# First stage of a hybrid retention and gMLP kernel: squares of x and context taken in the feature layout, and the first loads in another order

## The chip, the cores and the metric

The kernel runs on one core of a Trainium2 chip. The metric is the device time of one execution in microseconds. A second number, the span, is the time from the first to the last instruction of a profiled execution.

## The reference

The model has two layers over 512 latent tokens x and 256 context tokens ctx, each of 1024 features. Layer 0 mixes tokens by bidirectional retention, layer 1 by a chunked gMLP. The part that matters here is the beginning of layer 0: both streams are normalised over their features, modulated by vectors made from `c` and `c_ctx`, and multiplied with the input weights.

```python
def rmsnorm(x, g):
    xf = x.astype(F32)
    y = xf * lax.rsqrt(jnp.mean(xf * xf, axis=-1, keepdims=True) + NORM_EPS)
    return (y * g.astype(F32)).astype(x.dtype)
...
        shift_x, scale_x, gate_x = jnp.split(silu_c @ ada_w[i] + ada_b[i], 3, axis=-1)
        shift_c, scale_c, gate_c = jnp.split(silu_cc @ ada_w[i] + ada_b[i], 3, axis=-1)
        hx = rmsnorm(x, norm_g[i]) * (1 + scale_x[:, None]) + shift_x[:, None]
        hc = rmsnorm(ctx, norm_g[i]) * (1 + scale_c) + shift_c
...
    q = to_heads(h @ w_in[:, :a], RET_HEADS)
    k = to_heads(h @ w_in[:, a:bq], RET_HEADS) * (RET_QK_DIM ** -0.5)
```

So each token needs the sum of its 1024 squared features, and each feature needs a scale and a shift.

## The kernel before, in words

**Layout.** x and ctx lie with features on the partitions: 1024 features are eight blocks of 128, called kb (0 to 7), and tokens run along the free axis. x stands in four tiles `xq[th, g]` (128 x 4 x 256): th is the half of the tokens, g the half of the feature blocks. ctx stands in two tiles `cq[g]`. Layer 0's modulation weights come in eight pairs `ada_w[kb]`, 1 MB each.

**Precision.** Every float32 operand is cut into a high part (type fp32r, made by ScalarE, `act.copy` or an activation) and a low part (made by VectorE, source minus high part), and `mm3` (line 110) makes a product of three TensorE instructions: low times high, high times low, high times high. So each operand needs one pass of ScalarE and one of VectorE before TensorE can use it. In `features` (line 306) the first of the three needs the low part of the weights and the high part of x, the second needs the low part of x.

**The first stage** (lines 419 to 766) makes k and q of head 0 as a plain product: for each kb and each token half th, 12 TensorE instructions (`plain(kb, th)`, line 664), for the context 6. Around a block stand: `ada0_mm(kb)` (line 535), eight float32 products of the modulation with `ada_w[kb]`, and a copy by ScalarE; `ada0_cols(kb, e)` (line 545), two transposes that turn the result to the partitions, then a reduce and three small instructions on VectorE that leave scale `gs0` and shift `sh0`; `come(...)` (line 639), which scales a block of x or ctx by scale and reciprocal root (VectorE), adds the shift and makes the high part (ScalarE) and the low part (VectorE). The weight pieces of head 0 are items 0 to 3 of the stream `Q` (line 139); `Q.upto(n)` cuts items into high and low parts, 128 x 1024 at a time. Its tiles `hl` have four buffers, so items 4 and 5, the first of the second stage, take buffers that items 0 to 3 leave.

**The sums of squares** (`flips` and `squares`, lines 510 to 519): TensorE transposes 128 x 128 pieces of x into PSUM so that tokens lie on the partitions, and ScalarE squares them with a running sum per partition. `inverse` (line 521) adds the two halves, takes the root and the reciprocal; `spread` (line 526) multiplies a broadcast of the 128 reciprocals with the identity matrix so that they lie along the free axis on every partition, and ScalarE copies the result to `rs[th]`. The two halves of x are treated one after the other (`by_half`), the context's flips stand behind blocks 2 and 3, its spread behind block 4, and its blocks go through `come` and `plain` in the groups of `CTX_COME` and `CTX_PLAIN` (lines 729, 730).

**What sets the order.** In this stage `pe`, `act` and `dve` keep the order of the text (`kept`, lines 419 and 480, until line 766): each instruction of TensorE, ScalarE and VectorE goes behind the one before it in the text. Afterwards only TensorE does, and a scheduler orders the other two. Loads go out on SyncE's queue in the order of the text (`load`, line 128), those of `Q` when a slot is free (`pump`). `fill(n)` (line 464) issues n products of ones that nobody reads. Nearly every instruction is recorded at line 55, the helper that issues it.

The second stage begins with head pair (0, 1) of v, in the trace the first products of the form pst<-hl,oA.

Of the kernel before, what the change touches and what calls it, by code (L numbers as in the profile page):

```python
# [14 lines left out]
P = 128  # L15
D = 1024
# [52 lines left out]
def hybrid_kernel(ctx, tc, xT_d, cT_d, cv_d, sv_d, rows_d, ada0_d, adag_d, w_d, rope_d, dec_d, ws_d, id_d, out_d):  # L69
# [69 lines left out]
    class Stream:  # L139
# [3 lines left out]
        def __init__(self):  # L143
            self.items, self.loads, self.raws, self.left, self.tiles = [], [], {}, {}, {}
            self.free, self.stage, self.done, self.sent, self.at = [], 0, 0, 0, -1
            self.gate = self.limit = self.cap = None

# [10 lines left out]
        def load(self, key, slots, stage, parts):  # L158
            self.loads.append((key, slots, stage, parts))

# [274 lines left out]
    ADA_AT = ("oS1", "oS2", "oS4", "oA22", "oS1", "oS2", "oS4", ("w4", "g1"))  # L435
# [12 lines left out]
    load(xq[0, 0], xT_d[:, 0:4, 0:HS])  # L448
    load(ident, id_d)
    load(xq[0, 1], xT_d[:, 4:8, 0:HS])  # L450
    load(sv, sv_d)
    ada0_load(0)
    Q.stage = 1
    Q.pump_n(1)
    load_x(1)
    Q.pump_n(1)
    for kb in (1, 2, 3):
        ada0_load(kb)
    for g in range(2):
        load(cq[g], cT_d[:, 4 * g:4 * g + 4, :])  # L460
# [49 lines left out]
    def squares(pq, s):  # L510
        act.activation(t2("junk0"), pq, AF.Square, accum_out=s)

    def flips(src, g, i, s):

        pq = pt()
        for k in range(4):
            pe.transpose(pq[:, k * P:k * P + P], src(4 * g + k, i), ident)
        squares(pq, s[:, g, i:i + 1])
        return pq

    def inverse(s):
        dve.tensor_tensor(s[:, 0, :], s[:, 0, :], s[:, 1, :], ALU.add)
        act.activation(s[:, 1, :], s[:, 0, :], AF.Sqrt, bias=eps, scale=1.0 / D)
        dve.reciprocal(s[:, 1, :], s[:, 1, :])

    def spread(s, name):

        pr = pt((P, HS), tag="tm")
        for i in range(2):
            mm(pr[:, i * P:i * P + P], s[:, 1, i:i + 1].to_broadcast([P, P]), ident, start=True, stop=True)  # L530
# [14 lines left out]
    def ada0_cols(kb, e):  # L545
# [6 lines left out]
        dve.tensor_tensor(gs0[:, kb, :], s[:, 0, :], adab0[:, 1, kb, :], ALU.add)  # L552
        dve.tensor_tensor(sh0[:, kb, :], s[:, 1, :], adab0[:, 0, kb, :], ALU.add)
        dve.scalar_tensor_tensor(gs0[:, kb, :], gs0[:, kb, :], 1.0, g0[:, kb, :], ALU.add, ALU.mult)
# [70 lines left out]
    def half_rows(src, g, s):  # L625
        for i in range(2):
            flips(src, g, i, s)

    def by_half(src, name, n=0):
        s = sq[name] = st([P, 2, 2], f"sq{name}", name="sq")  # L630
        for g in range(2):
            half_rows(src, g, s)
            if g == 0:
                fill(n)
# [62 lines left out]
    for low in lows:  # L697
        low()
# [927 lines left out]
```

## Time and profile before

| what | value |
|---|---|
| runs of before, median (lowest to highest) | 875.29 us (875.2 to 875.54) |
| the profiled execution: time | 875.18 us |
| the profiled execution: span | 873.4 us |
| TensorE busy | 862.0 us, 99% of the span |
| VectorE busy | 708.6 us, 81% |
| ScalarE busy | 472.3 us, 54% |
| loads and stores | 153.80 MB, mean 176 GB/s |
| mean granted TensorE clock | 0.999 |

In a row of the timeline stand the start in us, the duration, the engine, the line, the operation, the output and its inputs, the shape and the count, and in brackets how long the engine was idle before and what ended that. PE is TensorE's matrix product, PEld its weight load, DVE is VectorE, ACT ScalarE, SPq SyncE's queue of loads. The trace shows a float32 product as two PE and two PEld records. In a row of stretches stand the stretch, its length, the busy time of PE, PEld, DVE, ACT and POOL with counts, then the granted clock, the share of the DMA engines and GB/s. In a row of groups stand the count, the busy time, the mean duration in ns and the idle time before.

### The profile page before, as it was taken

The page shows a single profiled execution, that of the slowest core. Times are in us where ns is not written, and L with a number is a line of the kernel's source. Part 1 is how long each engine was busy: PE and PEld are TensorE (multiplying, and loading weights), DVE is VectorE, ACT ScalarE, POOL GpSimd, SP SyncE. Part 2 cuts the span into 40 slices and gives each one's busy share as a digit, 9 for nine tenths or more (in the row PEclk, how much of TensorE's full clock was granted, in tenths as well). Part 3 has the DMA queues.
Part 4 walks back from the last instruction along what each step waited for, and adds up shares of the span by engine and source line. Part 5 has one row for each costly group of instructions (what it writes and reads, how often), then busy time and mean ns, then how long its engine had stood idle before and what let it go on. Part 6 is the DMA issues. An engine that isn't in the chain of part 4 may idle for free.

```text
span 873.4 us, 14635 instructions
## 1 busy us (share of the span) xinstructions
PE 862.0 (99%) x5670; PEld 777.3 (89%) x5670; DVE 708.6 (81%) x998; ACT 472.3 (54%) x763; POOL 62.6 (7%) x100
## 2 busy tenths in 40 slices
PE   8999999999999999999999999999999999999996
PEld 6898899898889888999989898888999899899895
DVE  2689979988696987878688869978898578779976
ACT  5466444553524576536362559785865455255345
POOL 0000210110121020000000010102000000000200
PEclk9999999999999999999999999999999999999999
DMA  9941761972695596758175722446435045045602
GB/s 332 393 136 62 241 219 59 301 253 97 213 370 145 192 314 220 258 167 303 42 254 188 232 85 77 146 167 217 146 122 176 17 146 191 7 142 194 94 28 97
DMA packets 77094, 153.80 MB, mean 176 GB/s; under 512 B 8032, under 2 KB 35040, under 8 KB 77024
## 3 DMA queue, kind: packets, MB, share of 16 engines
q1 hardware_dynamic: 68736, 128.53, 44.6%
q0 software_dynamic: 8000, 24.13, 8.4%
q8 instruction: 44, 0.72, 0.3%
q14 instruction: 26, 0.21, 0.1%
q10 hardware_dynamic: 288, 0.20, 0.1%
HBM read 128.71 MB, written 24.12 MB: 175 GB/s over the span
## 4 chain that ended last, share of the span: by engine, by line
PE 93%; ACT 2%; DVE 2%; DMA 2%; issue 0%; SPq 0%; ACTq 0%
PE pst L55 93%; DMA xq<-in_xT_dram 2%; DVE hl L55 1%; ACT hl L55 1%; ACT f L55 1%; ACT oA L55 0%; ACT junk L55 0%; DVE o L55 0%; DVE xq L55 0%; ACT o L55 0%; DVE cq L55 0%; DVE raw L55 0%; ACT oS L55 0%; DVE gs L55 0%; ACT fss L55 0%
## 5 line engine op out<-in xcount | busy, mean ns | idle before, releaser
L55 DVE TENSOR_TENSOR hl<-raw,hl 128x1024 fp32r<-128x1024 f32 x195 | 237.3, 1223 | 71.8 <-ACT hl L55 71.1
L55 ACT CAST hl<-raw 128x1024 fp32r<-128x1024 f32 x195 | 203.6, 1049 | 156.9 <-DVE raw L55 63.1
L55 PE MATMUL pst<-oS,hl 128*128 128x256 f32 x1104 | 134.1, 280 | 0.5 <-ACT oS L55 0.4
L55 PE MATMUL pst<-hl,oS 128*128 128x512 f32 x576 | 134.2, 390 | 0.1
L55 PEld LDWEIGHTS pst<-oS,hl 128*128 128x128 f32 x1104 | 130.9, 188 | 1.3 <-ACT oS L55 0.9
L55 PEld LDWEIGHTS pst<-hl,oS 128*128 128x128 f32 x576 | 107.9, 188 | 23.2 <-DVE oS L55 0.5
L55 PE MATMUL pst<-oA,hl 128*128 128x256 f32 x936 | 117.8, 281 | 0.2
L55 PEld LDWEIGHTS pst<-oA,hl 128*128 128x128 f32 x936 | 112.7, 188 | 2.4 <-issue 0.4
L55 DVE TENSOR_TENSOR raw<-raw 128x1024 f32<-128x1024 f32 x92 | 111.5, 1222 | 0.9
L55 PE MATMUL pst<-hl,oA 128*128 128x512 f32 x408 | 95.8, 390 | 0.0
L55 PE MATMUL pst<-og,hl 128*128 128x256 f32 x768 | 92.8, 280 | 0.0
L55 PEld LDWEIGHTS pst<-og,hl 128*128 128x128 f32 x768 | 90.9, 188 | 0.8 <-issue 0.4
L55 PEld LDWEIGHTS pst<-hl,oA 128*128 128x128 f32 x408 | 76.2, 188 | 15.5
L55 ACT COPY snap<-pst 128x512 f32<-128x512 f32 x84 | 49.1, 585 | 43.0 <-PE pst L55 41.9
L55 PE MATMUL pst<-hl,ya 128*128 128x512 f32 (+1 forms) x300 | 68.5, 381 | 0.0
L55 PEld LDWEIGHTS pst<-hl,ya 128*128 128x128 f32 x300 | 54.6, 188 | 10.7
L55 PE MATMUL pst<-v,ph 128*128 128x512 f32 x192 | 59.4, 391 | 0.0
L55 DVE TENSOR_TENSOR snap<-pst,snap 128x512 f32<-128x512 f32 x63 | 42.8, 688 | 5.7 <-PE pst L55 5.5
L55 ACT CAST ph<-pf 128x512 fp32r<-128x512 f32 x24 | 14.9, 620 | 52.1 <-DVE pf L55 49.7
L55 PEld LDWEIGHTS pst<-v,ph 128*128 128x128 f32 x192 | 36.1, 188 | 7.0
L55 DVE SCALAR_TENSOR_TENSOR acc<-pst,gate,acc 128x256 f32<-128x256 f32 x64 | 29.1, 480 | 13.6 <-PE pst L55 13.4
L55 PE MATMUL pst<-v,pl 128*128 128x512 f32 x96 | 37.9, 395 | 0.0
(196 smaller groups left out, 1011.9 us busy)
## 6 DMA issues: line engine op xcount, KB each, us to landing
raw<-in_w_dram SPq DMA_DIRECT2D x224, 256.0 KB, 4.2
bg<-in_adag_dram SPq DMA_DIRECT2D x32, 512.0 KB, 5.3
ada_w<-in_ada_dram SPq DMA_DIRECT2D x16, 512.0 KB, 8.7
raw<-in_w_dram SPq DMA_DIRECT2D x16, 512.0 KB, 3.7
bg<-in_dec_dram SPq DMA_DIRECT2D x12, 512.0 KB, 5.5
v<-snap POOLq DMA_DIRECT2D x16, 256.0 KB, 4.8
z<-snap POOLq DMA_DIRECT2D x16, 256.0 KB, 5.6
v<-v SPq DMA_DIRECT2D x8, 512.0 KB, 4.7
```

The costliest lines, as they stand in the source:

```text
L55: made = op(*args, **kw)
```

## The change

The squares are taken where the data lie, with features on the partitions. Of each tile of x, ScalarE squares two of the four blocks and VectorE the other two (a product of the tile with itself), and VectorE adds the two results into one tile of 128 x 512. TensorE then multiplies 128-column pieces of that tile, as weights, with one column of ones; the sums of 128 tokens come out as one PSUM column. Both halves of x are treated before anything else. The context's two tiles are treated the same in block 4, with two more additions on VectorE that leave 128 x 256, so that two products are enough.

The loads come in the order x (all four tiles), ada_w(0), block 0 of the first two weight pieces, ada_w(1), block 1 of them, ada_w(2), blocks 2 and 3, ada_w(3), ada_w(4), then the rest; identity and small vectors come on ScalarE's queue. `begin` loads such a part of two weight pieces, and `halve` cuts it into high and low parts. For blocks 0 and 1, `ready` multiplies x by its reciprocal root before the scale is known, and `first_come` does the rest, with the scale in ScalarE's activation.

```diff
+        def begin(self, ks, parts):
...
+                load(self.raws[key].rearrange("p (s n) -> p s n", s=2)[:, :, k0:k1],
+                     w_d[b:b + 2, :, kh * 512 + k0:kh * 512 + k1].rearrange("s p n -> p s n"))
+
+        def halve(self, i, ks, late=None):
...
+            split((part(hl[:, 0, :]), part(hl[:, 1, :])), part(self.raws[q, at]), late)
...
-    def squares(pq, s):
-        act.activation(t2("junk0"), pq, AF.Square, accum_out=s)
...
+    def squares(src):
...
+        act.activation(two(y[0]), src[:, 0:2, :], AF.Square)
+        dve.tensor_tensor(two(y[1]), src[:, 2:4, :], src[:, 2:4, :], ALU.mult)
+        dve.tensor_tensor(y[0], y[0], y[1], ALU.add)
+        return y[0]
+
+    def sums_of(y, banks, first, last):
+        n = y.shape[1] // HS
+        for k in range(n):
+            for i in range(2):
+                mm(banks[i][:, 0:1], y[:, k * HS + i * P:k * HS + i * P + P], ones[:, 0:1], start=first and k == 0,
+                   stop=last and k == n - 1, skip_group_check=True)
+
+    def inverse(banks, name):
+        r = st([P, 2], name, name="root")
+        for i in range(2):
+            act.activation(r[:, i:i + 1], banks[i][:, 0:1], AF.Sqrt, bias=eps, scale=1.0 / D)
+        dve.reciprocal(r, r)
+        return r
...
+    def ready(kb, th):
+
+        y = early[kb, th] = t2("early", (P, HS))
+        dve.tensor_tensor(y, xq[th, 0][:, kb, :], rs[th], ALU.mult)
+
+    def first_come(kb, th, lows=()):
...
+        act.activation(h, y, AF.Identity, bias=sh0[:, kb, 0:1], scale=gs0[:, kb, 0:1])
+        for low in lows:
+            low()
+        dve.tensor_scalar(f, y, gs0[:, kb, 0:1], None, ALU.mult)
+        dve.scalar_tensor_tensor(l, f, sh0[:, kb, 0:1], f32(h), ALU.add, ALU.subtract)
...
+    fill(2)
+    for th in range(2):
+        sq[th] = [pt() for i in range(2)]
+        for g in range(2):
+            sums_of(squares(xq[th, g]), sq[th], g == 0, g == 1)
+            fill(2)
+    for th in range(2):
+        sq[th] = inverse(sq[th], f"sq{th}")
+    for th in range(2):
+        rs[th] = spread(sq[th], f"rs{th}")
+    ready(0, 0)
+    ready(0, 1)
     es = ada0_mm(0)
...
+    Q.halve(0, (0,))
+    first_come(0, 0)
+    Q.halve(1, (0,), lows)
+    first_come(0, 1, lows)
...
+    first_come(1, 0)
+    first_come(1, 1)
+    for i in (0, 1):
+        Q.halve(i, (1,))
...
-    CTX_COME = {4: (0, 1, 2), 5: (3, 4), 6: (5, 6, 7)}
-    CTX_PLAIN = {5: (0, 1, 2), 6: (3, 4), 7: (5, 6, 7)}
+    CTX_COME = {5: (0, 1, 2), 6: (3, 4, 5), 7: (6, 7)}
+    CTX_PLAIN = {6: (0, 1, 2), 7: (3, 4, 5, 6, 7)}
...
+        if kb == 1:
+            for i in (0, 1):
+                Q.halve(i, (2, 3))
+        if kb in (2, 3, 6, 7):
+            Q.upto({2: 3, 3: 4, 6: 5, 7: 6}[kb])
+        if kb == 4:
+            y = [squares(cq[g]) for g in range(2)]
+            dve.tensor_tensor(y[0], y[0], y[1], ALU.add)
+            dve.tensor_tensor(y[0][:, 0:HS], y[0][:, 0:HS], y[0][:, HS:], ALU.add)
         plain(kb, 1)
-        if kb + 2 < 8:
+        if kb < 6:
             es = ada0_mm(kb + 2)
...
-        if kb in (2, 3):
-            half_rows(rows_c, kb - 2, sq[2])
...
         if kb == 4:
+            sq[2] = [pt((P, HS), tag="tm") for i in range(2)]
+            sums_of(y[0][:, 0:HS], sq[2], True, True)
+            sq[2] = inverse(sq[2], "sq2")
+        if kb == 5:
             rs[2] = spread(sq[2], "dec")
```

How this moves instructions is shown at three places. In these rows oA and oS with a number are the parts of x for the first and second token half, ident,cq are flips of the context, adae the turn of the modulation, ada_w its products, hc the context. First TensorE, before, from the modulation in block 2 to the start of block 4:

```order
L55 MATMUL pst<-ada_w,cpad 32x256 x8
L55 MATMUL pst<-ident,cq 128x128 x8
L55 MATMUL pst<-oA_250,hl 128x256 x12
L55 MATMUL pst<-ident,adae 128x128 x2
L55 MATMUL pst<-oS_308,hl 128x256 x12
L55 MATMUL pst<-ada_w,cpad 32x256 x8
L55 MATMUL pst<-ident,cq 128x128 x8
L55 MATMUL pst<-oA_555,hl 128x256 x12
```

And TensorE after, block 4 and the start of block 5:

```order
L55 MATMUL pst<-oA_535,hl 128x256 x12
L55 MATMUL pst<-ident,adae 128x128 x2
L55 MATMUL pst<-oA_537,hl 128x256 x12
L55 MATMUL pst<-ada_w,cpad 32x256 x8
L55 MATMUL pst<-ones,squares 128x1 x2
L55 MATMUL pst<-oA_535,hl 128x256 x12
```

The 16 flips of the context are gone; two products with the context's squares stand between the modulation in block 4 and block 5.

VectorE at the same place, before, from block 4's x (the rows that begin with xq) to the reduce of the next block:

```order
L55 SCALAR_TENSOR_TENSOR xq<-xq,gs_151,rs_240 128x256
L55 SCALAR_TENSOR_TENSOR xq<-xq,gs_151,rs_306 128x256
L55 SCALAR_TENSOR_TENSOR oA_555<-xq,sh_152,oA_555 128x256
L55 SCALAR_TENSOR_TENSOR oA_557<-xq,sh_152,oA_557 128x256
L55 TENSOR_TENSOR sq<-sq 128x2
L55 RECIPROCAL sq<-sq 128x2
L55 TENSOR_REDUCE ada_s<-pst 128x4
```

VectorE after, from block 5's x, which `come` makes within block 4:

```order
L55 SCALAR_TENSOR_TENSOR xq<-xq,gs_155,rs_250 128x256
L55 SCALAR_TENSOR_TENSOR xq<-xq,gs_155,rs_255 128x256
L55 SCALAR_TENSOR_TENSOR oA_535<-xq,sh_156,oA_535 128x256
L55 SCALAR_TENSOR_TENSOR oA_537<-xq,sh_156,oA_537 128x256
L55 TENSOR_TENSOR squares<-cq 128x512
L55 TENSOR_TENSOR squares<-squares 128x512
L55 TENSOR_TENSOR squares<-cq 128x512
L55 TENSOR_TENSOR squares<-squares 128x512 x2
L55 TENSOR_TENSOR squares<-squares 128x256
L55 RECIPROCAL root<-root 128x2
L55 TENSOR_REDUCE ada_s<-pst 128x4
```

Six instructions on the context's squares stand behind block 5's x and ahead of the reciprocal and of the reduce of the next block.

The end of the stage on VectorE, before, from the low part of the second stage's first weight piece (hl) to the sum of x for that stage:

```order
L55 TENSOR_TENSOR hl<-raw,hl 128x1024
L55 SCALAR_TENSOR_TENSOR cq<-cq,gs_151,dec 128x256 x3
L55 SCALAR_TENSOR_TENSOR hc<-cq,sh_152,hc 128x256 x3
L55 TENSOR_TENSOR hl<-raw,hl 128x1024
L55 TENSOR_TENSOR xq<-xq 128x1024
```

The same after:

```order
L55 TENSOR_TENSOR hl<-raw,hl 128x1024
L55 SCALAR_TENSOR_TENSOR cq<-cq,gs_155,dec 128x256 x3
L55 SCALAR_TENSOR_TENSOR hc<-cq,sh_156,hc 128x256 x3
L55 TENSOR_TENSOR hl<-raw,hl 128x1024
L55 SCALAR_TENSOR_TENSOR cq<-cq,gs_155,dec 128x256 x2
L55 SCALAR_TENSOR_TENSOR hc<-cq,sh_156,hc 128x256 x2
L55 TENSOR_TENSOR xq<-xq 128x1024
```

Two blocks of the context come behind the second weight piece. On TensorE the last context products are 30 in a row behind block 7, where 12 stood ahead of block 7 and 18 behind it.

More of the change, by code (lines that the diff above doesn't have):

```diff
@@ L146, in __init__ @@
             self.gate = self.limit = self.cap = None
+            self.begun = {}
         def quad(self, q, names, place=None):
@@ L159, in load @@
             self.loads.append((key, slots, stage, parts))
+        def begin(self, ks, parts):
+            k0, k1 = ks[0] * P, ks[-1] * P + P
+            for i, (b, kh) in enumerate(parts):
+                key, slots, stage = self.loads[i][:3]
+                if ks[0] == 0:
+                    self.free.remove(slots[i])
+                    self.raws[key] = st([P, 1024], slots[i], name="raw")
+                    self.left[key] = [slots[i], sum(it[0] == key[0] and key[1] in it[2] for it in self.items)]
+                    self.sent += 1
+                load(self.raws[key].rearrange("p (s n) -> p s n", s=2)[:, :, k0:k1],
+                     w_d[b:b + 2, :, kh * 512 + k0:kh * 512 + k1].rearrange("s p n -> p s n"))
+        def halve(self, i, ks, late=None):
+            q, name, uses, at, place = self.items[i]
+            if ks[0] == 0:
+                self.tiles[i] = self.begun[i] = split_tile(q[0])
+                self.done += 1
+            part = lambda x: x.rearrange("p (s n) -> p s n", s=2)[:, :, ks[0] * P:ks[-1] * P + P]
+            hl = self.begun[i]
+            split((part(hl[:, 0, :]), part(hl[:, 1, :])), part(self.raws[q, at]), late)
+            if ks[-1] == 3:
+                self.drop(q, uses)
         def pump_n(self, n):
@@ L434, in hybrid_kernel @@
     ada_w = {}
[L435 removed]
+    ADA_AT = ("oS1", "oS2", "oS4", "oA22", ("w4", "g1"), "oS1", "oS2", "oS4")
     def ada0_load(kb):
@@ L447, in hybrid_kernel @@
     nc.scalar.dma_start(cv, cv_d)
[L448 to L451, printed above, removed]
+    nc.scalar.dma_start(ident, id_d)
+    nc.scalar.dma_start(sv, sv_d)
+    load_x(0)
+    load_x(1)
     ada0_load(0)
[L453 to L460, printed above, removed]
+    Q.stage, Q.cap = 1, 2
+    FIRST = ((2, 0), (0, 0))
+    Q.begin((0,), FIRST)
+    ada0_load(1)
+    Q.begin((1,), FIRST)
+    ada0_load(2)
+    Q.begin((2, 3), FIRST)
+    ada0_load(3)
+    ada0_load(4)
     warm = pt()
@@ L508, in hybrid_kernel @@
     sh0 = st([P, KT, 2], "sh0")
-    def squares(pq, s):
-        act.activation(t2("junk0"), pq, AF.Square, accum_out=s)
[L513 to L524, printed above, removed]
+    def squares(src):
+        y = [t2("squares") for j in range(2)]
+        two = lambda t: t.rearrange("p (k n) -> p k n", k=2)
+        act.activation(two(y[0]), src[:, 0:2, :], AF.Square)
[14 more added lines that the diff above has]
+        return r
     def spread(s, name):
@@ L529, in spread @@
         for i in range(2):
-            mm(pr[:, i * P:i * P + P], s[:, 1, i:i + 1].to_broadcast([P, P]), ident, start=True, stop=True)
+            mm(pr[:, i * P:i * P + P], s[:, i:i + 1].to_broadcast([P, P]), ident, start=True, stop=True)
         rs = st([P, HS], name)
```

63 lines of the change are left out of this document (20 added, 43 removed).

## The prediction

> **What bounds the kernel now.** The page comes first (span and busy time by engine), then the busy time by stretches, then who waited for whom on TensorE's weight loads after 60 us.
>
> ```profile
> span 873.4 us, 14635 instructions
> PE 862.0 (99%) x5670; PEld 777.3 (89%) x5670; DVE 708.6 (81%) x998; ACT 472.3 (54%) x763; POOL 62.6 (7%) x100
> ```
>
> ```profile
> 0.00:15.70 15.70, 12.28 (x92) 10.49 (x93) 3.38 (x12) 9.29 (x23) 0.20 (x4) 1.00 0.88 302
> 15.70:24.08 8.38, 7.78 (x75) 5.64 (x73) 4.73 (x13) 4.41 (x11) 0.00 (x0) 1.00 1.03 409
> 59.63:873.40 813.77, 806.67 (x5181) 729.96 (x5179) 675.58 (x904) 440.04 (x689) 62.44 (x96) 1.00 0.51 166
> ```
>
> ```profile
> PEld pst L55 <- issue: 1.7, 5, 0.4
> ```
>
> TensorE (PE) is the bound: 862.0 of 873.4 us. The first 15.70 us hold 12.28 us of it, much of that filler; from 59.63 us, where the second stage begins, no single kind of wait of its weight loads totals over 1.7 us. So the change is worth what it does to the moment at which the second stage's first product starts, 59.63 us, and I carry that shift to the end unchanged. The execution took 875.18 us for its span of 873.4, and the median of the runs is 875.29; I add the shift to 875.2. About 0.2%, 1.75 us, is what a measurement can tell from no change.
>
> The weight loads of TensorE show the stage's beat best, since they show real gaps:
>
> ```profile
> 28.30 1.47 PEld L55 LDWEIGHTS pst<-oA,hl 128*128 128x128 f32 x12 [0.41 <-ACT oS L55]
> 29.71 0.25 PEld L55 LDWEIGHTS pst<-ident,adae 128*128 128x128 f32 x2
> 29.93 1.47 PEld L55 LDWEIGHTS pst<-oS,hl 128*128 128x128 f32 x12
> 31.53 0.59 PEld L55 LDWEIGHTS pst<-ada_w,cpad 128*32 128x32 f32 x16
> 32.53 0.86 PEld L55 LDWEIGHTS pst<-ident,cq 128*128 128x128 f32 x8 [0.41 <-DMA ada_w<-in_ada_dram]
> 33.36 1.47 PEld L55 LDWEIGHTS pst<-oA,hl 128*128 128x128 f32 x12
> ...
> 37.59 0.86 PEld L55 LDWEIGHTS pst<-ident,cq 128*128 128x128 f32 x8 [0.41 <-issue]
> 38.42 0.19 PEld L55 LDWEIGHTS pst<-oA,hl 128*128 128x128 f32 x1
> 38.94 1.35 PEld L55 LDWEIGHTS pst<-oA,hl 128*128 128x128 f32 x11 [0.33 <-DVE oA L55]
> ```
>
> One block kb without context work: twelve products of the first half 1.41, the turn of the modulation 0.22, twelve of the second half 1.60, the modulation of a later block 1.00, in all 4.23 us (28.30 to 32.53). Context flips cost 0.83 twice (32.53 to 33.36, and 37.59 to 38.42), and block 4 waits 0.33 for VectorE. VectorE's part of a block:
>
> ```profile
> 30.24 0.17 DVE L55 TENSOR_REDUCE ada_s<-pst 128x4 f32<-128x16 f32 x1 [1.68 <-PE pst L55]
> ...
> 30.84 0.88 DVE L55 SCALAR_TENSOR_TENSOR xq<-xq,gs,rs 128x256 f32<-128x256 f32 x2
> 31.90 0.48 DVE L55 SCALAR_TENSOR_TENSOR oA<-xq,sh,oA 128x256 fp32r<-128x256 f32 x1 [0.18 <-ACT oA L55]
> 32.30 0.48 DVE L55 SCALAR_TENSOR_TENSOR oS<-xq,sh,oS 128x256 fp32r<-128x256 f32 x1
> ```
>
> It starts 1.94 us after the block's first product (30.24 less 28.30), because it needs the turn on TensorE, and could take other work from about 32.70, 4.40 us after it.
>
> **Step 1: the start.** The trace has no such order of loads; the nearest row is this one:
>
> ```profile
> 10.32 0.64 PE L55 MATMUL pst<-ada_w,cpad 128*32 128x256 f32 x8 [0.56 <-DMA ada_w<-in_ada_dram]
> 14.86 0.86 PEld L55 LDWEIGHTS pst<-ident,xq 128*128 128x128 f32 x8 [0.63 <-DMA xq<-in_xT_dram]
> ```
>
> Before, the loads up to the second half of ada_w(0) are cv, ident, sv, two quarters of x and 1 MB of ada_w: 2,176 KB, landed at 10.3. The change has loaded exactly as many when the fourth quarter of x is in, so x is complete at L = 10.3 instead of 14.86 (bounds 9.6 to 11.0, as narrow rows may come slower). Behind that quarter stand:
>
> ```profile
> L55 DVE TENSOR_TENSOR rope_a<-held,rope 128x512 f32<-128x512 f32 x4 | 2.7, 687 | 0.0
> L55 DVE TENSOR_TENSOR rope_a<-rope_a,rope_b 128x256 f32<-128x256 f32 x32 | 12.2, 422 | 0.3
> L55 ACT ACTIVATE sq<-sq,eps 128x2 f32<-128x2 f32 x3 | 0.9, 296 | 0.5 <-DVE sq L55 0.5
> L55 DVE TENSOR_SCALAR o<-o,fss 128x512 f32<-128x512 f32 x3 | 1.5, 485 | 0.1
> ```
>
> ```profile
> 17.38 0.17 DVE L55 RECIPROCAL sq<-sq 128x2 f32<-128x2 f32 x1 [0.36 <-ACT sq L55]
> 17.60 0.52 PEld L55 LDWEIGHTS pst<-ident,sq 128*128 128x128 f32 x4
> 18.35 0.37 ACT L55 COPY rs<-pst 128x256 f32<-128x256 f32 x1
> ```
>
> Multiply and add on VectorE, 2 x 0.69, with hand-overs 1.45; four products with the column of ones. No row shows such a product; the nearest is the spread, where two products with 128-column weights load in 0.52, so 1.04 with 0.1 to leave (bounds 0.5 and 1.2). By the Trainium skill, "TensorE: Matmul & The Clock Gate", section "LDWEIGHTS (loading the stationary operand)", a load goes by its columns, about 107 ns for 128; eight loads would then be an estimated 0.86, and the sum 0.2 us less at the start and 0.1 less at block 4. Then two roots 0.5, the reciprocal 0.2, the spread 0.65: ada_w(0) can enter TensorE at L + 3.95 (its own 1 MB lands before). Modulation 1.15, copy 0.37, turn and hand-over 0.52: VectorE's first reduce stands at R = L + 6.0 = 16.3. Scale, shift, the low part of the first weight piece (0.42), the scaling of x (half of the 485 ns row at least, the whole at most; I take 0.33) and the low part of x (0.48) put the first dense products at R + 1.8 = 18.1, against 15.7 for a lone six before.
>
> From there TensorE has 12 products, modulation 1, six products and turn 1, which puts reduce 1 at R + 5.3. It reaches block 1 at R + 6.7, but the new pieces of weights are cut on VectorE behind two scalings and two low parts and come at R + 8.1: a wait of 1.4. In block 2 the two 128x512 pieces (0.69 each) stand behind the four instructions of x, reduce 2 + 3.35, where TensorE comes at + 2.3: 1.05 more. Block 2 begins at R + 13.4 and block 3 a beat later, R + 17.6 = 33.9. Before, block 3 began at 33.36, after one flip of the context. Taken: **+0.6 us** (bounds -1.0 and +2.0). The loads keep up: TensorE asks for ada_w(1) at R + 3.1, 19.4, and the 2.36 MB up to it behind x take 5.8 us after 10.3 at the 409 GB/s of the row 15.70:24.08, 7.8 at the 302 of the first; ada_w(2), 1.31 MB more, is asked for at 22.3 and is there at 19.3 by the one rate, 22.4 by the other.
>
> **Step 2: flips gone.** The second flip, 0.83, and the 0.33 wait behind it go: **-1.15 us**.
>
> **Step 3: the context's sum.** TensorE's queue now holds two products with the squares between modulation 6 and block 5. VectorE makes these squares in its queue behind the x part of block 5, which itself waits for the turn of block 5. With block 4's first product as zero: VectorE is free at 4.40; five 128x512 instructions at 0.69 and one of 0.42 make 3.87, so the sum is ready at 8.3. The flips before were TensorE's own work; here TensorE ends modulation 6 at 4.23 and can do nothing else, since its queue keeps the order of the text. That is a wait of **+4.1 us** (3.6 if they follow each other at 0.60, 4.5 with late hand-overs), and then two products, **+0.5** (0.2 to 0.6). What queues behind it: block 5 on TensorE, and through it VectorE's next reduce.
>
> **Step 4: the tail.**
>
> ```profile
> 43.49 1.48 PEld L55 LDWEIGHTS pst<-oA,hl 128*128 128x128 f32 x12
> ...
> 57.06 0.19 PEld L55 LDWEIGHTS pst<-hc,hl 128*128 128x128 f32 x1
> 57.63 2.07 PEld L55 LDWEIGHTS pst<-hc,hl 128*128 128x128 f32 x17 [0.38 <-DVE hc L55]
> 59.63 0.54 PEld L55 LDWEIGHTS pst<-hl,oA 128*128 128x128 f32 x3
> ```
>
> ```profile
> 44.20 1.27 DVE L55 SCALAR_TENSOR_TENSOR cq<-cq,gs,dec 128x256 f32<-128x256 f32 x3 [0.85 <-ACT dec L55]
> ...
> 46.58 0.17 DVE L55 TENSOR_REDUCE ada_s<-pst 128x4 f32<-128x16 f32 x1
> ```
>
> ```profile
> 54.77 1.23 DVE L55 TENSOR_TENSOR hl<-raw,hl 128x1024 fp32r<-128x1024 f32 x1 [0.45 <-ACT hl L55]
> 55.91 1.27 DVE L55 SCALAR_TENSOR_TENSOR cq<-cq,gs,dec 128x256 f32<-128x256 f32 x3
> 56.42 1.31 ACT L55 ACTIVATE hc<-cq,sh 128x256 fp32r<-128x256 f32 x3 [1.69 <-DVE cq L55]
> 57.10 1.27 DVE L55 SCALAR_TENSOR_TENSOR hc<-cq,sh,hc 128x256 fp32r<-128x256 f32 x3
> ```
>
> The context's blocks come one kb later, and thirty of its products instead of eighteen stand at the end. Zero is now block 6's first product, which follows the context's spread as 43.49 does here. As there, context blocks 0 to 2 are made first and the reduce comes at 3.1, so x's last part ends at 5.6, the weight piece's low part at 7.3, and blocks 3 to 5 of the context have their low parts at 8.9, 9.3 and 9.7. TensorE is through with block 7 at 8.0: a wait of 0.9. Then VectorE must cut the second weight piece (cast to 10.0, low part to 11.25) before context blocks 6 and 7, whose low parts end at 12.7 and 13.1; TensorE is through with block 5 of the context at 10.9: 1.7 more. Before, this place cost 0.45 beyond the pace of 0.118 per product. **+2.1 us** (1.0 to 2.8).
>
> **Sum:** 0.6 - 1.15 + 4.1 + 0.5 + 2.1 = 6.15; 875.2 + 6.15 = 881.3 us.
>
> **The rivals.** *Covered waits, faster.* If VectorE has the context's sum within 4.2 us of block 4's start instead of 8.3, so that both queues keep ahead of TensorE, only the gains stay: blocks 1 and 2 without their 2.45 us, +0.6 becoming -1.85, the flip and wait -1.15, two products +0.5, the old tail wait of 0.45 gone: -2.95, 872.2 us. For it: VectorE is busy only 3.38 of the first 15.70 us. Against it: the six instructions alone take 3.87 and cannot start before the turn. 6%.
>
> *One of the two late waits is not there* (most likely the tail's, where one weight piece's slot decides the order): 881.3 less 2 to 4, 877.2 to 879.3. 14%.
>
> *TensorE slows after its wait.* The filler products show two paces:
>
> ```profile
> 1.06 4.12 PE L55 MATMUL pst<-ones 128*128 128x128 f32 x20 [1.06 <-DVE eps L55]
> ...
> 6.29 1.28 PE L55 MATMUL pst<-ones 128*128 128x128 f32 x10
> ```
>
> 0.206 us each at first, 0.128 later, though the granted clock reads 1.00 throughout. If the wait of 4.1 us brings the first pace back for another 4.1, work of 2.6 us takes 4.1: +1.6, 882.9 us. The Trainium skill, "TensorE: Matmul & The Clock Gate", section "Part 1: The HAM clock gate (the "warmup" mystery)", states that one idle window of about 3.4 us halves the clock; the window runs freely, so a wait of 4.1 holds a whole one only sometimes. The trace agrees on the slow start, and has no wait that long to test the fall back. 16%.
>
> *The change does nothing* (the second stage starts within 1.75 us of where it did): needs a front shorter by its whole bound and half the waits; 4%.
>
> **How the numbers follow.** Forecast 60%: 881.3, its own range 878.6 to 883.5 from the bounds of the four steps, not all at one end. Slower pace 16%, one wait missing 14%, no change 4%, faster 6%. Leaving out the last two and the thinnest edges, 877.8 to 884.5 holds 8 in 10. Faster 0.06, same 0.04, slower 0.90.
>
> **What would show it.** Step 1: x's last quarter at about 10.3, the first product with oA at about 18, waits of TensorE for VectorE's hl pieces of some 1.4 and 1.0, block 3 at 34. Step 3: TensorE's longest wait after 20 us is for VectorE's squares, about 4 us near 42. Step 4: waits for hc of 0.9 and 1.7, the second stage at about 65.7. I am wrong if the products with squares start without a wait, or if the second stage starts by 61.

## The result, and the profile after

The changed kernel takes 889.76 us (median of four runs, 889.39 to 891.63); the kernel before took 875.34 beside it on the same chip. The ratio is 1.0169, 95% interval 1.0151 to 1.0186: 14.4 us slower. The prediction (881.3, range 877.8 to 884.5) had the sign and the size of three of its five terms (flips, the context's wait, the tail), and was too small by 8.5 us. The profiled execution is the slowest of the four, 891.63 us for a span of 889.8, so its terms add up to about 2 us more than the median's.

The page first, and the busy time by stretches:

```profile
span 889.8 us, 14630 instructions
PE 870.7 (98%) x5656; PEld 784.6 (88%) x5656; DVE 718.8 (81%) x1017; ACT 470.1 (53%) x752; POOL 62.6 (7%) x100
PEclk7989999999999999999999999999999999999999
```

```profile
0.00:15.70 15.70, 14.08 (x72) 13.55 (x73) 6.23 (x13) 6.42 (x13) 0.20 (x4) 0.79 0.91 308
15.70:24.00 8.30, 6.93 (x44) 4.99 (x43) 4.03 (x14) 2.82 (x7) 0.00 (x0) 0.71 1.04 392
76.30:889.80 813.50, 806.52 (x5181) 729.72 (x5179) 674.31 (x903) 440.08 (x688) 62.44 (x96) 1.00 0.51 166
```

From the second stage on nothing has changed: 813.50 us here, 813.77 before, both with 5181 matrix products at clock 1.00. The loss lies ahead of it, since the second stage starts at 76.30 us instead of 59.63: +16.67. What is new in the start is the column behind the five engines, the granted clock: 0.79 and 0.71, where both stretches before read 1.00. TensorE is busy for more of the first stretch than before (14.08 us against 12.28) and issues fewer instructions in it (72 against 92).

TensorE's weight loads show the beat, block by block:

```profile
30.73 1.47 PEld L55 LDWEIGHTS pst<-oA,hl 128*128 128x128 f32 x12 [1.85 <-DVE hl L55]
35.98 1.47 PEld L55 LDWEIGHTS pst<-oA,hl 128*128 128x128 f32 x12 [1.43 <-DVE hl L55]
40.23 1.47 PEld L55 LDWEIGHTS pst<-oA,hl 128*128 128x128 f32 x12 [0.41 <-ACT oS L55]
...
44.45 0.77 PEld L55 LDWEIGHTS pst<-oA,hl 128*128 128x128 f32 x6 [0.41 <-ACT oA L55]
46.43 0.76 PEld L55 LDWEIGHTS pst<-oA,hl 128*128 128x128 f32 x6 [1.22 <-DVE hl L55]
...
54.31 0.93 PEld L55 LDWEIGHTS pst<-ones,squares 128*128 128x128 f32 x4 [4.76 <-issue]
55.12 2.68 PEld L55 LDWEIGHTS pst<-oA,hl 128*128 128x128 f32 x12
...
62.22 1.48 PEld L55 LDWEIGHTS pst<-oA,hl 128*128 128x128 f32 x12
...
70.57 0.19 PEld L55 LDWEIGHTS pst<-hc,hl 128*128 128x128 f32 x1 [0.26 <-ACT hc L55]
71.22 2.06 PEld L55 LDWEIGHTS pst<-hc,hl 128*128 128x128 f32 x17 [0.46 <-DVE hc L55]
74.51 0.19 PEld L55 LDWEIGHTS pst<-hc,hl 128*128 128x128 f32 x1 [1.23 <-ACT hc L55]
75.03 1.35 PEld L55 LDWEIGHTS pst<-hc,hl 128*128 128x128 f32 x11 [0.33 <-DVE hc L55]
76.30 2.59 PEld L55 LDWEIGHTS pst<-hl,oA 128*128 128x128 f32 x12
```

Blocks 1, 2 and 3 start at 30.73, 35.98 and 40.23. Block 4 is split by a wait of 1.22 for a weight piece (hl). Ahead of the context's sums TensorE is idle for 4.76 us ("issue", but what ends it is VectorE's last addition, below). Then look at the durations: twelve loads of block 5 take 2.68, where blocks 1 to 3 have 1.47. The clock explains that. Before, and then after:

```profile
8.00:10.00 2.00, 1.17 (x13) 0.48 (x11) 0.16 (x1) 1.26 (x4) 0.00 (x0) 1.00 1.01 379
```

```profile
9.00:19.30 10.30, 10.30 (x57) 8.85 (x56) 3.82 (x8) 2.79 (x8) 0.00 (x0) 0.51 1.05 383
...
54.00:62.00 8.00, 7.66 (x48) 6.97 (x49) 2.66 (x10) 1.43 (x4) 0.00 (x0) 0.60 0.01 2
```

After the change TensorE runs at half clock for ten microseconds from 9.2 us, for 3.4 us more from 22.9, and again from 53.6 to 60.4, most of block 5. In the first of these stretches the profile calls it busy all the time (10.30 of 10.30), while before it kept clock 1.00 with a busy time of 1.17 out of 2. The same eight loads for a group of sums show the step, and so does VectorE's work around the waits:

```profile
6.78 0.97 PEld L55 LDWEIGHTS pst<-ones,squares 128*128 128x128 f32 x8 [0.72 <-DVE squares L55]
13.01 1.83 PEld L55 LDWEIGHTS pst<-ones,squares 128*128 128x128 f32 x8
...
45.16 1.23 DVE L55 TENSOR_TENSOR hl<-raw,hl 128x1024 fp32r<-128x1024 f32 x1 [0.45 <-ACT hl L55]
...
50.13 0.68 DVE L55 TENSOR_TENSOR squares<-cq 128x512 f32<-128x512 f32 x1
...
52.32 1.88 DVE L55 TENSOR_TENSOR squares<-squares 128x512 f32<-128x512 f32 x3
```

The weight piece for which block 4 waits ends on VectorE at 46.39 (45.16 + 1.23), and block 4's second six loads start at 46.43. The six instructions on the context's squares run from 50.13 to 54.20 (52.32 + 1.88, the short one of 128x256 counted among the three), and the sums start at 54.31: the predicted queue, one after the other.

The shift of 16.67 us, by the prediction's own terms:

| term | forecast | in this trace | how |
|---|---|---|---|
| start of block 3 | +0.6 | +6.9 | 40.23 against 33.36 |
| flips and the wait behind them | -1.15 | -1.15 | block 3 to 4: 4.22 against 5.06; the 0.33 does not recur |
| late weight piece in block 4 | none | +1.2 | wait 1.22 for hl |
| wait for the context's squares | +4.1 | +4.35 | 4.76 less the usual 0.41 |
| the two products | +0.5 | +0.8 | 55.12 less 54.31, at half clock; 0.44 at full clock in experiment 4 |
| block 5 at half clock | a rival, +1.6 | +2.4 | 62.22 less 55.12 is 7.10; 4.68 at full clock in experiment 4 |
| tail | +2.1 | +2.2 | 62.22 to 76.30 is 14.08; before, without a block of 4.23, 59.63 less 43.49 less 4.23 = 11.91 |

The right column adds up to 16.7.

### The profile page after: what moved, and what is told of

Its sections match the earlier page's. It is cut to its first block, busy times and chain, and to the rows that moved or that the text cites. A ratio compares the mean times of both kernels' runs of the same rounds, so it can differ in the third digit from the quotient of the medians.

```text
span 889.8 us, 14630 instructions
## 1 busy us (share of the span) xinstructions
PE 870.7 (98%) x5656; PEld 784.6 (88%) x5656; DVE 718.8 (81%) x1017; ACT 470.1 (53%) x752; POOL 62.6 (7%) x100
## 4 chain that ended last, share of the span: by engine, by line
PE 92%; DVE 4%; ACT 3%; issue 0%; DMA 0%; ACTq 0%; DVEq 0%
PE pst L55 92%; DVE hl L55 1%; ACT hl L55 1%; ACT oA L55 1%; DVE squares L55 1%; ACT f L55 0%; DVE o L55 0%; DMA cv<-in_cv_dram 0%; DVE xq L55 0%; ACT junk L55 0%; DVE gs L55 0%; DVE cq L55 0%; DVE oA L55 0%; DVE hc L55 0%; ACT hc L55 0%
## 5 line engine op out<-in xcount | busy, mean ns | idle before, releaser
L55 DVE TENSOR_TENSOR hl<-raw,hl 128x1024 fp32r<-128x1024 f32 (+2 forms) x199 | 237.5, 1200 | 71.4 <-ACT hl L55 70.8
L55 ACT CAST hl<-raw 128x1024 fp32r<-128x1024 f32 (+2 forms) x199 | 204.3, 1031 | 160.3 <-DVE raw L55 62.9
L55 PE MATMUL pst<-oA,hl 128*128 128x256 f32 x936 | 121.1, 286 | 4.2 <-DVE hl L55 3.3
L55 PEld LDWEIGHTS pst<-oA,hl 128*128 128x128 f32 x936 | 115.7, 193 | 7.5 <-DVE hl L55 4.5
```

Source lines behind the costliest of these rows:

```text
L55: made = op(*args, **kw)
```

## The experiments

Each kernel below is timed against the kernel before on its own chip; the times are medians, and the ratios are to that before. Theory at the outset: the sums' products with a single column let the clock fall in the start, and the wait for the context's squares lets it fall again. The rivals: the start is long for another reason (loads, VectorE), or the gaps alone make the clock fall, whatever the products are.

**1. Wide products.** The sums are multiplied with all 128 columns of ones instead of one; only the first column of the result is read.

```diff
-                mm(banks[i][:, 0:1], y[:, k * HS + i * P:k * HS + i * P + P], ones[:, 0:1], start=first and k == 0,
+                mm(banks[i][:, 0:P], y[:, k * HS + i * P:k * HS + i * P + P], ones, start=first and k == 0,
```

> The changed kernel with one edit: the products that sum the squares use all 128 columns of ones instead of one, same number of products. Theory A (TensorE's clock falls to half from 9.3 us because one-column products keep the array nearly idle while the queue looks busy): granted clock 1.00 through the first 30 us, first product of x with weights near 18.3 instead of 22.4 us, block 3 near 36 instead of 40.2, time 4 to 5.5 us below the changed kernel's 889.8, about 885. Rival B (the clock falls because too little filler stands between, whatever the products' width, or the start is late by its chain): clock falls as before, time within 1 us of 889.8.

886.19 us (885.85 to 886.97), ratio 1.0129 (1.0113 to 1.0146): 3.6 us less than the changed kernel, from products that do more arithmetic. That is a little under the 4 to 5.5 of theory A; the two profiled executions, 891.63 and 886.29, are 5.3 apart. Its weight loads and one stretch of the start:

```profile
34.75 1.47 PEld L55 LDWEIGHTS pst<-oA,hl 128*128 128x128 f32 x12 [0.41 <-ACT oS L55]
...
48.84 0.93 PEld L55 LDWEIGHTS pst<-ones,squares 128*128 128x128 f32 x4 [4.76 <-issue]
49.64 2.68 PEld L55 LDWEIGHTS pst<-oA,hl 128*128 128x128 f32 x12
```

```profile
9.00:10.00 1.00, 1.00 (x11) 1.00 (x10) 0.90 (x3) 0.63 (x1) 0.00 (x0) 1.00 1.05 388
```

In the second from 9 to 10 us TensorE gets through 11 matrix instructions at clock 1.00, where the changed kernel made 7 at 0.62, and block 3 starts at 34.75, 5.5 us earlier. The wait of 4.76 stands as it was, with wide products behind it, and block 5 is slow all the same. So the two falls have different triggers: the width of the sums in the start, the wait in block 4.

**2. More filler between one-column sums.** Five products of ones instead of two behind each group of sums.

```diff
             sums_of(squares(xq[th, g]), sq[th], g == 0, g == 1)
-            fill(2)
+            fill(5)
```

> The changed kernel with five filler products instead of two behind each group of sum products in the start, one-column products kept. Theory A (what counts is how much the array streams: more filler keeps the clock as wide products do): clock 1.00 up to the context's wait, time about 886.3 as with wide products. Rival B (one-column products let the clock fall whatever stands between): clock 0.50 from about 9 us, 889.8 or 0.5 more.

896.19 us (894.79 to 898.18), ratio 1.0242 (1.0228 to 1.0256), 6.4 us more than the changed kernel.

```profile
8.19 1.31 PEld L55 LDWEIGHTS pst<-ones 128*128 128x128 f32 x10
9.38 1.83 PEld L55 LDWEIGHTS pst<-ones,squares 128*128 128x128 f32 x8
11.09 2.25 PEld L55 LDWEIGHTS pst<-ones 128*128 128x128 f32 x10
...
20.90 1.83 PEld L55 LDWEIGHTS pst<-ident,root 128*128 128x128 f32 x8
```

Ten loads of filler take 1.31 and then 2.25: the clock falls at the same place, although more than half the time there now goes to wide filler. It stays down for as long as the groups alternate, and the filler, slow itself, now lies on the chain: the spread starts at 20.90. Filler beside the one-column products does not hold the clock; other products in their place do. Rival B was right about the clock and too low on the price, since it left out that chain.

**3. The context's part alone.** The kernel before with only the second half of the change: squares of the context on ScalarE and VectorE, its two products in block 4, its blocks one kb later. x keeps its flips.

```diff
+        if kb == 4:
+            y = [squares_c(cq[g]) for g in range(2)]
...
-        if kb in (2, 3):
-            half_rows(rows_c, kb - 2, sq[2])
-        if kb == 3:
-            inverse(sq[2])
         if kb == 4:
...
+            sums_of(y[0][:, 0:HS], sq[2], True, True)
```

> The kernel before with the context's part of the change alone (squares on VectorE and ScalarE, sums by two products, the later groups of context blocks), x as before. Theory A: flips and wait gone -1.15, wait +4.2, products +0.6, slow clock +2.4, tail +2.1: 8.1 us above before, 883.4, so that x's part is the other 6 us. Rival B (the context's part costs only what was predicted, without the clock): +5.5, 880.9, and x's part costs 9. Rival C (x's part is most of it): below +4.

883.38 us (882.25 to 883.6), ratio 1.0093 (1.0078 to 1.0108): +8.2 (theory A had 8.1), which leaves about 6.2 of the 14.4 to the part with x and the loads. The wait is the same 4.76:

```profile
45.63 0.93 PEld L55 LDWEIGHTS pst<-ones,squares 128*128 128x128 f32 x4 [4.76 <-issue]
46.44 2.68 PEld L55 LDWEIGHTS pst<-oA,hl 128*128 128x128 f32 x12
```

Block 5 is at half clock here too, so the second fall needs nothing from the start. The other half of the change adds the rest on top of it.

**4. Filler within the wait.** The changed kernel with 15 products of ones, which nobody reads, ahead of the context's sums.

```diff
+            for n in range(15):
+                mm(sq[2][0][:, P:], ones, ones, start=True, stop=True, skip_group_check=True)
             sums_of(y[0][:, 0:HS], sq[2], True, True)
```

> The changed kernel with 15 filler products of ones (about 3.8 us) ahead of the context's two sum products, in the time when TensorE waits. Theory A (the wait itself brings the slow clock): the sums start when they did, the clock stays 1.00 behind them, block 5 takes 4.7 instead of 7.1 us, time 2.4 us lower, about 887.4. Rival B (the slow clock has another cause, such as the one-column products): block 5 still at half clock, time as the changed kernel's or 0.3 longer.

888.93 us (887.4 to 891.25), ratio 1.0162 (1.0144 to 1.0179). That is only 0.8 under the changed kernel, and the intervals overlap, so the time alone decides nothing. The trace does for its own execution; these are the first loads of blocks 5 and 6:

```profile
54.84 1.48 PEld L55 LDWEIGHTS pst<-oA,hl 128*128 128x128 f32 x12
...
59.52 1.47 PEld L55 LDWEIGHTS pst<-oA,hl 128*128 128x128 f32 x12
```

Block 5 takes 4.68 us, where the changed kernel took 7.10. Its start was at half clock like the changed kernel's, and how long that lasts differs from execution to execution: the mean clock is 0.988 in the slowest of the four and 0.992 in the fastest.

**5. Both: wide products and filler within the wait.** The edits of 1 and 4 together.

> The changed kernel with both edits that kept the clock: sum products 128 columns wide, and 15 filler products in the context's wait. Theory A (the clock is all that the forecast missed besides one wait of 1.2): granted clock 1.00 everywhere, block 5 takes 4.7 instead of 7.15 us, 2.8 us below the wide kernel's 886.2, so 883.4, which is the forecast's 881.3 and the 1.2 wait and about 1 more in the start. Rival B (something else slows the first stage): 885 or more with the clock at 1.00.

884.12 us (883.59 to 884.82), ratio 1.0103 (1.0089 to 1.0117): 2.1 less than wide products alone.

```profile
49.23 1.47 PEld L55 LDWEIGHTS pst<-oA,hl 128*128 128x128 f32 x12
```

Block 5's first twelve loads are back at 1.47, and in this execution the clock stays at 1.00 through the whole first stage. Two of the four executions kept it (883.63 and 883.59, mean clock 0.998 and 0.999); the other two (884.60 and 884.82) have a mean clock of 0.996, which points to a short fall in them. With the clock kept the change still costs 8.3 us, 883.6 less 875.28; that is the cost of its waits and of its longer start.

**6. The order of the late weight pieces.** Kernel 5, with the fourth weight piece's low part cut one block earlier, and the second stage's second piece behind the last blocks of the context.

```diff
-        if kb in (2, 3, 6, 7):
-            Q.upto({2: 3, 3: 4, 6: 5, 7: 6}[kb])
+        if kb in (2, 6):
+            Q.upto({2: 4, 6: 5}[kb])
...
         come(*((k, 2) for k in CTX_COME.get(kb, ())))
+        if kb == 7:
+            Q.upto(6)
```

> The kernel with wide products and filler in the wait, and two cuts of weight pieces moved in the text: the second piece of feature half 2 from block 3 to block 2, the second stage's second piece behind the last context blocks. Theory A (these two are the waits of 1.2 in block 4 and of 1.6 ahead of context block 6): both gone, 2.3 to 2.8 us lower than without, about 880.9. Rival B (VectorE's queue is full there, the waits only move to block 3 or to the second stage): less than 1 us lower.

881.69 us (881.13 to 882.81), ratio 1.0078 (1.0063 to 1.0094): 2.4 less.

```profile
61.82 0.19 PEld L55 LDWEIGHTS pst<-hc,hl 128*128 128x128 f32 x1 [0.24 <-ACT hc L55]
62.47 3.60 PEld L55 LDWEIGHTS pst<-hc,hl 128*128 128x128 f32 x29 [0.46 <-DVE hc L55]
66.00 2.58 PEld L55 LDWEIGHTS pst<-hl,oA 128*128 128x128 f32 x12
```

The 29 loads of the context run through without the waits of 1.23 and 0.33, and the 1.22 in block 4 is gone too, with 0.47 and 0.28 in its place in blocks 3 and 4.

**7. The sums one block later.** The changed kernel, with the context's two products behind block 5's second half, ahead of the last modulation.

```diff
         plain(kb, 1)
+        if kb == 5:
+            sq[2] = [pt((P, HS), tag="tm") for i in range(2)]
+            sums_of(y[0][:, 0:HS], sq[2], True, True)
+            sq[2] = inverse(sq[2], "sq2")
...
-        if kb == 4:
-            sq[2] = [pt((P, HS), tag="tm") for i in range(2)]
-            sums_of(y[0][:, 0:HS], sq[2], True, True)
-            sq[2] = inverse(sq[2], "sq2")
```

> The changed kernel with the context's two sum products moved behind block 5 on TensorE instead of ahead of it. Theory A (the wait is TensorE's queue held by VectorE's six squares, and the slow clock behind it follows from that wait): the 4.3 us wait shrinks to about 0.7, a wait of some 0.6 appears ahead of the last modulation because both small PSUM buffers are held, the clock stays 1.00 from 40 to 65 us, time about 5.4 us lower, 884.4. Rival B (the wait only moves, since VectorE's queue is the limit there): no more than 1.5 us lower.

887.64 us (886.59 to 889.25), ratio 1.0146 (1.0131 to 1.0161): 2.1 less than the changed kernel, under half of what the cover of a whole block should bring. The waits of TensorE and one later stretch:

```profile
54.18 0.52 PEld L55 LDWEIGHTS pst<-ones,squares 128*128 128x128 f32 x4 [1.26 <-issue]
56.20 0.20 PEld L55 LDWEIGHTS pst<-ada_w,cpad 128*32 128x32 f32 x8 [1.50 <-ACT root L55]
```

```profile
57.00:58.00 1.00, 1.00 (x12) 0.20 (x4) 0.00 (x0) 0.00 (x0) 0.00 (x0) 0.50 0.00 0
```

The long wait is gone. A short one is left ahead of the sums, and a new one behind them, where the modulation waits for ScalarE's root. Neither reaches 1.6 us, yet the clock falls at 55.5 us. So neither theory holds as it stood: the wait is covered as theory A said, but two waits of twice its size are left (1.26 and 1.50 for 0.7 and 0.6), and the clock is not kept.

**8. The same with wide products.** The edits of 1 and 7.

> The changed kernel with both earlier edits: all sum products with 128 columns of ones, and the context's two sum products behind block 5's second half, ahead of modulation 7. Question: why did the clock fall between 55 and 63 us with the products moved, although no wait was longer than 1.5 us? Theory A, the two one-column products between the waits of 1.26 and 1.50 do not count for the clock, so that 53.1 to 56.2 is one gap of 3.1: with wide products the clock stays at 1.00 to the second stage; against the wide products alone (886.2) 2.4 less for block 5 at full clock and 2.0 less for the shorter waits (4.76 against 1.26 + 1.50), about 881.8. Theory B, two waits of 1.3 and 1.5 close to each other are enough: the clock falls to 0.5 near 55 all the same, and the time stays at 884 or more.

882.34 us (882.11 to 883.33), ratio 1.0086 (1.0071 to 1.0102). The time is near the first theory's 881.8, but in the profiled execution its reason is not borne out: the clock does fall, as theory B had it.

```profile
48.17 0.52 PEld L55 LDWEIGHTS pst<-ones,squares 128*128 128x128 f32 x4 [1.26 <-issue]
50.19 0.51 PEld L55 LDWEIGHTS pst<-ada_w,cpad 128*32 128x32 f32 x12 [1.50 <-ACT root L55]
```

```profile
52.00:53.00 1.00, 1.00 (x7) 1.00 (x6) 0.00 (x0) 0.37 (x1) 0.00 (x0) 0.50 0.16 52
...
54.00:55.00 1.00, 1.00 (x11) 1.00 (x11) 1.00 (x4) 0.87 (x3) 0.00 (x0) 1.00 0.00 0
```

Two gaps of 1.26 and 1.50 with a half microsecond of wide products between them were enough here. They are not always: of the eight executions of this kernel and the next, five have a mean granted clock of 0.998 or 0.999, like the profiled kernels without a fall (before, 5 and 6), and three, both profiled ones among them, 0.995 or 0.996. The clock is back to 1.00 after 3.4 us, where the one-column version needed 6.8. Behind the fall TensorE is busy for 3.42 of the next 3.42 us here and for 2.72 of 3.41 there; that this is the reason is not shown.

**9. Late sums, wide, order mended.** The edits of 1, 6 and 7 without filler.

> The same, with the order of the late weight pieces mended as before: the low part of the fourth weight piece ahead of block 3's second half, the second weight piece of the second stage behind the last blocks of the context. Theory A (clock kept, both late waits for weight pieces gone): 2.4 less than the kernel without this order, about 879.4, second stage near 63.8. Theory B (the clock falls in block 6, or the context's late spread now makes a wait of its own): 881 or more.

879.56 us (879.16 to 881.81), ratio 1.0058 (1.0044 to 1.0071): the best version of the change, and still 4.5 us slower than before. The profiled execution is the slowest of its four, 881.81, and shows by what:

```profile
7.54 1.71 PEld L55 LDWEIGHTS pst<-ones,squares 128*128 128x128 f32 x8 [2.23 <-DVE squares L55]
```

```profile
8.00:9.00 1.00, 1.00 (x7) 1.00 (x6) 0.90 (x2) 0.24 (x1) 0.00 (x0) 0.50 1.15 372
```

The first filler ended sooner here, TensorE waited 2.23 us for the first squares, and the clock fell at once, with wide products behind the gap. It fell again for 3.4 us at 52.0, behind the two late gaps as in 8. This execution took 2.1 us more than the next of the four, 879.75; its mean clock is 0.995, that of the other three 0.998 or 0.999.

**10. The kernel before with only its context flips replaced, additions on GpSimd.** ScalarE squares the context in block 1, GpSimd adds, two wide products stand behind block 3. One addition of a single column on GpSimd at the start of the kernel comes with it.

```diff
+        nc.gpsimd.tensor_tensor(a, a, b, ALU.add)
...
+        if kb == 1:
+            square(0)
+            square(1)
...
+                mm(pc[:, i * HS:i * HS + P], yc[0][:, i * P:i * P + P], ones, start=True, stop=True, skip_group_check=True)
```

> The kernel before, x as before, with the context's 16 flips replaced: ScalarE squares all context blocks in block 1, GpSimd adds them, two products 128 columns wide stand where the second flip stood, all else in before's order. Theory A (the idea is sound where the queue that makes the sums has room and time): flips -1.66, products +0.5, 1.0 to 1.4 us lower than before, about 874.0. Rival B (GpSimd is too slow for four additions in 8 us, TensorE waits at block 3's end): 875.2 or more.

877.14 us (876.77 to 877.59), ratio 1.0021 (1.0012 to 1.003). The flips are gone, and TensorE waits instead. GpSimd and VectorE side by side, then TensorE:

```profile
30.26 2.53 POOL L736 TENSOR_TENSOR squares<-squares 128x512 f32<-128x512 f32 x2 [28.96 <-ACT squares L55]
```

```profile
31.60 1.20 DVE L55 SCALAR_TENSOR_TENSOR gs<-gs,sv 128x2 f32<-128x2 f32 x1
32.84 2.44 DVE L55 SCALAR_TENSOR_TENSOR xq<-xq,gs,rs 128x256 f32<-128x256 f32 x2
```

```profile
35.00 0.19 PEld L55 LDWEIGHTS pst<-oA,hl 128*128 128x128 f32 x1 [2.56 <-ACT oA L55]
```

While GpSimd adds, VectorE's instruction on two columns takes 1.20 us and the scaling of x 2.44, where the kernel before has 0.16 and 0.88 for the same two. The wait of 2.56 stands ahead of block 3, for its x; so rival B had the time, but not the place, since the sums behind block 3 were ready.

**11. The same with the additions on VectorE**, two in block 1 and two in block 2. The first half of ScalarE's squares moves from the end of block 1 to its middle.

```diff
+    def add(g):
+        dve.tensor_tensor(yc[2 * g], yc[2 * g], yc[2 * g + 1], ALU.add)
...
+        if kb == 1:
+            square(1)
+            add(0)
+            add(1)
+        if kb == 2:
+            dve.tensor_tensor(yc[0], yc[0], yc[2], ALU.add)
+            dve.tensor_tensor(yc[0][:, 0:HS], yc[0][:, 0:HS], yc[0][:, HS:], ALU.add)
```

> The kernel before, with the context's flips replaced by squares on ScalarE in block 1, additions on VectorE (two in block 1, two in block 2) and two products with 128 columns of ones behind block 3. Theory A, the loss of the version with additions on GpSimd came from VectorE slowing down beside GpSimd: VectorE's small instructions stay at 0.16 us, TensorE's wait of 2.56 is gone, second stage at 58.6 to 59.6 (59.63 before), time 874.3 to 875.3. Theory B, VectorE has no room for 2.5 us of additions in blocks 2 to 4: TensorE waits over 1 us for oA in block 3 or 4, second stage at 60.2 or later, 875.9 or more.

875.22 us (874.65 to 875.71), ratio 1.0002 (0.9994 to 1.0011): the same as before.

```profile
30.35 0.16 DVE L55 SCALAR_TENSOR_TENSOR gs<-gs,sv 128x2 f32<-128x2 f32 x1
```

```profile
37.95 0.19 PEld L55 LDWEIGHTS pst<-oA,hl 128*128 128x128 f32 x1 [1.18 <-ACT oA L55]
```

VectorE's small instruction is back at 0.16, so GpSimd's additions were what slowed it. But most of the 1.7 us that the flips took comes back as a wait of 1.18 in block 4, because VectorE reaches block 4's x hardly sooner than before. The second stage starts at 59.18, 0.45 us earlier; but block 1 already starts 0.57 earlier in this execution (23.51 against 24.08), ahead of all that the edit changes, so the edit itself gained nothing in it. Theory A has the cause and the time, theory B the wait in block 4. No version tried beats the kernel before by more than can be measured.

## Why the sign was right and the size wrong

**What bounds.** Right: from the second stage on both traces agree within 0.3 us, and the whole difference is the shift of its first product.

**Step 1, the start: the step that failed.** The prediction put the first dense products at 18.1 and block 3 at 33.9, +0.6. The trace has 21.86 for the first product with oA and 40.23 for block 3. Its pieces were sound: x's last quarter comes at about 10.4 (VectorE's last product of x, squares from xq, starts at 10.49), and the kernel with wide products has its first oA product at 17.95. What failed is the assumption, never stated, that TensorE keeps its full clock there. Every term was a duration taken from a place with clock 1.00. In the changed kernel the clock halves at 9.2 us for ten microseconds, and at 22.9 for 3.4 more. That is 5.5 of the 6.3 us by which block 3 is late beyond the forecast in the profiled execution (40.23 here, 34.75 with wide products), and 3.6 us by the medians (889.76 less 886.19). The other 0.85 are there with wide products too, 34.75 for 33.9. They are not the two waits for the weight pieces: 1.85 and 1.43 contain the 0.41 that stands ahead of other blocks as well, so 1.44 and 1.02 for 1.4 and 1.05. With wide products they gather ahead of block 1: VectorE's first reduce comes at 16.63 for 16.3, the second at 22.25 for 21.6, block 1 at 25.28 for 24.4. The sums' own loads were priced well: eight took 0.97 us while the clock was full, for 1.04 taken; at half clock they took 1.83. By the Trainium skill, "TensorE: Matmul & The Clock Gate", section "LDWEIGHTS (loading the stationary operand)", eight loads of 128 columns are an estimated 0.86; the 0.97 at full clock is near it.

**Step 2, flips gone.** Right, but it stopped one row too early, and this is the second term that the sum lacked. The 0.33 wait of block 4 is gone, and in its place stands one for the fourth weight piece, 1.22. Before, this piece was cut ahead of block 3; the change cuts it behind block 4's x, a line of the diff that the prediction did not follow to the reader of the piece.

**Step 3, the context's sum.** Right in mechanism and nearly in size: 4.35 us for 4.1, longest wait of the stage, six VectorE instructions in a row behind block 5's x. It came at 50 to 54 us instead of near 42, since all before it was late.

**Step 4, the tail.** Right: waits of 0.26 + 0.46 and 1.23 + 0.33 for context blocks, 2.2 more than before for 2.1 forecast.

**The rivals.** The wait did slow TensorE, at 16% the prediction's second likeliest case, and in every kernel here with the unfilled wait of 4.76 (the changed one, 1, 2 and 3). It cost 2.4 rather than 1.6, since the half clock lasted 6.8 us and not as long as the wait. It should have been a term of the sum: a wait of 4.1 was forecast, and a price for it was at hand. By the Trainium skill, "TensorE: Matmul & The Clock Gate", section "Part 1: The HAM clock gate (the "warmup" mystery)", the clock falls after an idle window of about 3.4 us that runs freely. From this the prediction concluded that a wait of 4.1 holds a whole one only sometimes. In the four profiled kernels with the wait of about 4.3 us the 3.41 us ahead of the fall hold 0.00 us of TensorE work, which agrees with the window; but "only sometimes" was too hopeful, since all four show the fall, and all eight executions of 1 and 3 have a mean clock of 0.992 to 0.994. Neither late wait was missing (14%), no wait was covered (6%).

What a corrected sum gives: where the clock was kept (experiment 5) the change costs 8.3 us, and the prediction's 6.15 with the late weight piece in block 4 (1.2) and the longer start (0.85) makes 8.2. So it was a fair sum of the waits at a clock that was not granted. The rest of the 14.4 is the clock, twice: 3.6 in the start (889.76 less 886.19) and 2.6 in block 5 (886.19 less 883.6). With the two late weight pieces mended as well (experiment 6) 6.4 are left; one of these two, the tail's, was in the 6.15.

What stays open: why one-column products let the clock fall. The runs show that their width decides it in the start, that filler beside them does not help, and at which times the clock can change (last section); they do not show what the chip counts.

## What to carry to other kernels

Read the granted clock of every stretch from which a duration is taken, and ask whether the changed stretch will be granted the same; a busy TensorE is no proof of it. Where TensorE would otherwise run little else for some microseconds, try a sum over partitions with many columns in place of one, even though only one is needed. Whatever moves work from a full queue (TensorE's flips) to another engine must be followed to the next reader on that engine's own queue, and each weight piece to the block that reads it.

## What the runs showed of the hardware

Full busy time and half clock can go together: 10.30 of 10.30 us busy at 0.51. All four profiled kernels with one-column sums in the start fell to half clock there (the changed one, 2, 4 and 7), and of the five with wide sums (1, 5, 6, 8, 9) only the ninth did, after a gap of 2.23 us. The gap ahead of the first sums does not explain this by itself: the clock fell with one column behind 0.72 (the changed kernel) and 1.25 us (2), and stayed with wide sums behind 1.05 (8), 1.60 (6), 1.63 (1) and 1.89 (5). In 4 and 7, with gaps of 1.92 and 1.88, the gap may have had its part.

The clock changed only in steps of 3.41 us: in each of the eight profiled kernels in which it fell, the times between any two changes are whole multiples of that, to about 0.02. The changed kernel falls at 9.24, 22.90 and 53.62 and is back at 19.48, 26.31 and 60.44, so the half clock lasted 3, 1 and 2 of these steps. This means that the 3.41 us ahead of a change can be laid beside others. The changed kernel ahead of its first fall, then experiment 8 at the same place, where the clock stayed:

```profile
5.83:9.24 3.41, 2.84 (x24) 2.46 (x22) 2.40 (x5) 1.09 (x3) 0.00 (x0) 1.00 1.09 352
```

```profile
6.00:9.41 3.41, 2.55 (x22) 2.36 (x22) 2.75 (x5) 1.68 (x3) 0.00 (x0) 1.00 1.11 353
```

The busier of the two is the one behind which the clock fell; its sums have one column. In all four kernels with one-column sums in the start, the clock came back at the end of the first whole step without such a sum (19.48; 22.87 in 2, 21.93 in 4, 21.37 in 7). Busy time alone does not decide among the other steps either: the changed kernel's 19.48 to 22.90, busy for 2.05 us, was followed by a fall, and one of experiment 8, 23.06 to 26.48, also busy for 2.05, was not.

Short gaps can do it as well, though not in every execution: 2.23 us in experiment 9, 1.26 and 1.50 in experiment 8 with 0.52 of products between. The Trainium skill, "TensorE: Matmul & The Clock Gate", section "Why this matters for your kernels", advises against idle gaps over about 3 us between bursts; these runs had the fall at gaps below that.

Adding on GpSimd slowed VectorE's instructions on two tiles of SBUF, from 0.16 to 1.20 and from 0.88 to 2.44 us (experiment 10), and the slowing went with the additions (11). The Trainium skill, "SBUF — State Buffer", section "Who interferes with whom", states this conflict for VectorE instructions with two SBUF inputs beside a GpSimd instruction that reads SBUF; the traces agree.
